# A two-layer mLSTM and RG-LRU trunk on one core: weight-block sums begun later, layer-border splits, sigmoid, gate matrix and head scores moved by half units

## The chip, the cores and the metric

The kernel runs on one core of one Trainium2 chip. The metric is device time in microseconds (us) of one execution. TensorE (PE in the profile) multiplies matrices, VectorE (DVE) and ScalarE (ACT) work elementwise, GpSimd (POOL) does small things and issues accumulating transfers, SyncE (SP) issues most other transfers.

## What is computed

Two layers (`DEPTH`), then a final RMSNorm. The input is 256 tokens of 2048 channels, all in float32.

```
u = rms_norm(x, norm_g)
qk, v, o, z_a, ig, fg, xb, z_b = split(u @ w_in)
qk = silu(causal_dwconv(qk)); q, k = split(qk)       # 8 heads, 128 channels each
h = mlstm_chunkwise(q, k, v, i_pre, log_f) * sigmoid(o)
y_a = head_norm(h) * silu(z_a)
y_b = rg_lru(causal_dwconv(xb) + b, w_a, w_x, lam) * silu(z_b)
x = x + concat(y_a, y_b) @ w_out
```

All but a few per cent of the arithmetic is `u @ w_in` (2048 by 12304) and `@ w_out` (4096 by 2048), twice.

## The kernel before

**Halves.** Float32 products are made of three products of a shorter type (fp32r): each weight tile is split into a rounded part wH and a rest wL, the activations likewise. The unit of work is a *half*: 128x1024 weights of a 1 MB tile `raw` that SP loads. ScalarE casts them to wH (L370), VectorE subtracts to get wL (L371), and TensorE makes 12 products of 512 columns (`mm_a`, L394). There are three `raw` buffers and four wH/wL pairs; a half is prepared three halves ahead (`AHEAD`), and `raw` can be loaded again when wL of its second half is done.

**Order.** `_sequence` lists the weight tiles: per layer four groups `g` of two heads, each with the chunks o, qk, v, xb, z, zb and a gate, and the output chunks of the group before. The loop at L1366 walks through the halves; at each it prepares a later one, emits the products, runs what is due in `timed` (L1392), and calls `pump` (L1395). `pump` advances the generators in `bg`, in which all the work between the products is written. What a generator yields decides: a number is a cost taken from the half's budget, `"wait"` means "not in this half, go on with the next generator", and `None` ends the pump of this half for every generator. Each engine then runs its instructions strictly in the order so made. Instructions that are emitted beside the products are put behind the splits of a certain half on their engine (`Behind`, L102, with `LAG` = 1: the split before the newest).

**Heads.** `qk_post` (L684) sends q and k through a transpose in DRAM (`moved`, `fr`), convolves (12 `qc` steps on VectorE), multiplies by a sigmoid (`qsg`), splits to `qks`, and for each of a group's two heads makes the scores: products into the PSUM tiles `ps_S` (L718, L720), copied and added to `Pt`, which is multiplied by the gate matrix E. Three PSUM banks (`aux`) serve these; a head needs two. `e_gen` (L630) makes E: it loads `nb` from DRAM by GpSimd's queue, yields `None` twice, adds and clips on VectorE (L644), and takes the exponential on ScalarE.

**Border of the layers.** The output chunk `c` of the last group (`out_chunk`, L961) gives the next layer's input: it is transposed through DRAM, and `split` (L1003), due `BORDER` = 7 halves later, scales it, casts it to `x_s` on ScalarE and subtracts on VectorE. The next layer's products read chunk c from the 16th + 4c-th half of the border on.

**Block products.** Two of the chunks, (z, 2) and (o, 3), are multiplied together by a scheme of seven 2x2 block products (`block_halves`, L1088) in place of eight. Their 28 halves per layer have six products each and stand spread between the ordinary ones, in a stretch that begins at `span[l]` (L1344). They need sums of weight blocks, which `weight_sums` (L1064) makes in DRAM: SP copies one block to `w_d` (L1074), GpSimd adds others to it with accumulating transfers (L1076), in quarters of 512 KB, `PACE` = 4 halves apart. It is begun with the first chunk of layer 0.

Of the kernel before, what the change touches and what calls it, by code (L numbers as in the profile page):

```python
# [11 lines left out]
AF = mybir.ActivationFunctionType  # L12
ALU = mybir.AluOpType
# [7 lines left out]
DEPTH = 2  # L21
# [7 lines left out]
LANDING = 4  # L29
BORDER = 7  # L30
BLANKS = 7
PACE = 4
BLOCKS_AHEAD = 5
LAG = 1

# [61 lines left out]
def tile_trunk(ctx, tc, x, xt, par, gw, gb, ws, final_g, out):  # L97
# [4 lines left out]
    class Behind:  # L102
# [4 lines left out]
        def __getattr__(self, name):  # L107
            f = getattr(self.engine, name)

            def g(*a, **k):  # L110
                ins = f(*a, **k)  # L111
                if st.get("behind"):
                    order(ins, done[self.key][-1 - LAG])
                return ins
            return g

# [513 lines left out]
    def e_gen(l, g):  # L630
        while ("nG", l) not in st:
            yield "wait"
        nb = work.tile([P, 2, T], F32, tag="sD", name="nb")
        src = nG_d[l][2 * g : 2 * g + 2, :].rearrange("h t -> (h t)").partition_broadcast(P)
        st["nb", l, g] = nc.gpsimd.dma_start(out=nb.rearrange("p h t -> p (h t)"), in_=src)
        yield None
        yield None
        while ("aT", l) not in st:
            yield "wait"
        E = small.tile([P, 2, 384], F32, tag="E", name="E", bufs=1)  # L640
        aT = st["aT", l]
        for h in range(2):
            hd = 2 * g + h
            ts_(E[:, h, 0:256], nb[:, h, :], aT[:, 0, hd : hd + 1], ALU.add, 0.0, ALU.min)  # L644
            ts_(E[:, h, 256:384], nb[:, h, 128:256], aT[:, 1, hd : hd + 1], ALU.add, 0.0, ALU.min)
        yield 0.7
        order(S.activation(out=E, in_=E, func=AF.Exp), st["wH"])
        for h in range(2):
            for o in (0, 256):
                G.affine_select(out=E[:, h, o : o + 128], in_=E[:, h, o : o + 128], pattern=[[1, 128]],  # L650
                                compare_op=ALU.is_ge, fill=0.0, base=0, channel_multiplier=-1)
        st["E", l, g] = E
        yield 0.1
# [30 lines left out]
    def qk_post(l, g, acc):  # L684
# [3 lines left out]
        def gen():  # L688
# [6 lines left out]
            for ct in range(4):  # L695
                conv(ch, qc, ct, O_QKW + 4 * (8 * (ct % 2) + 2 * g + ct // 2), l, None)
                yield 1.2
            S.activation(out=sg, in_=qc, func=AF.Sigmoid)
            tt_(qc, qc, sg, ALU.mult)
            yield 1.2  # L700
            while ("aT", l) not in st:
# [11 lines left out]
            for h in range(2):  # L713
                pa, pb = aux("ps_S"), aux("ps_S")
                kH, kL = q[:, 2 * h + 1, 0], q[:, 2 * h + 1, 1]
                for ps, ss_, ts_1 in ((pa, slice(0, 128), slice(0, 256)), (pb, slice(128, 256), slice(128, 256))):
                    n_ = ts_1.stop - ts_1.start
                    PE.matmul(ps[:, 0 : 2 * n_].rearrange("p (a t) -> p a t", a=2), kH[:, ss_], q[:, 2 * h, :, ts_1],  # L718
                              start=True, stop=False, skip_group_check=True)
                    PE.matmul(ps[:, 0:n_], kL[:, ss_], q[:, 2 * h, 0, ts_1], start=False, stop=True,  # L720
                              skip_group_check=True)
                for ps, o_, n_ in ((pa, 0, 256), (pb, 256, 128)):
                    S.copy(out=Pt[:, h, o_ : o_ + n_], in_=ps[:, n_ : 2 * n_])
                    tt_(Pt[:, h, o_ : o_ + n_], ps[:, 0:n_], Pt[:, h, o_ : o_ + n_], ALU.add)
                stt(Pt[:, h, :], Pt[:, h, :], DK_SCALE, E[:, h, :], ALU.mult, ALU.mult)
                yield 0.5
            st["scores", l, g] = True
            PH = work.tile([P, 2, 384], F32R, tag="sD", name="PH")
            PL = work.tile([P, 2, 384], F32R, tag="sC", name="PL")
# [231 lines left out]
    def out_chunk(l, g, c):  # L961
# [9 lines left out]
        def postfn():  # L971
            ps = acc()
            if g < NG - 1:
                stage = act.tile([P, 2, 512], F32, tag="stage", name="stage")
                S.copy(out=stage, in_=ps)
                st["gq"] = G.dma_start(out=xd[c], in_=stage, accum_op=ALU.add)
                return
            if c == 0:
                new_ss()
                new_xT()  # L980
                load_gw(l + 1)
            if c % 2:
                two = work.tile([P, 2, 1024], F32, tag="xcs", name="tokblk")
                tok = two[:, 0].rearrange("p (m c t j) -> p m c t j", m=4, c=4, t=2)
                blk = two[:, 1].rearrange("p (m n) -> p m n", m=4)
            else:
                tok, blk = new_tok(), None
            xs = xa(c)
            if c == 3:
                tt_(xs, xs, ps, ALU.add)  # L990
            for t in range(2):
                xt_ = xa(c, t).rearrange("p (c m j) -> p c m j", c=4, m=4)
                if c == 3:
                    S.copy(out=by_block(tok, t), in_=xt_)
                else:
                    tt_(by_block(tok, t), xt_, ps[:, t, :].rearrange("p (c m j) -> p c m j", c=4, m=4), ALU.add)
            if c < 3:
                tt_(xs, xs, ps, ALU.add)
            fr = swapped(tok, blk)
            square_sum(c)  # L1000
            store_x(c)

            def split():  # L1003
                xn = st["x_n"][:, 4 * c : 4 * c + 4]
                split_channels(fr, pars[:, l + 1, O_NG + 4 * c : O_NG + 4 * c + 4], xn[:, :, 0, :], xn[:, :, 1, :])
                st["xT", l + 1, c] = True
            timed.append((st["n"] + BORDER, split))

        for half_src in range(2):
            key = ("ya", l, g) if half_src == 0 else ("yb", l, g)  # L1010
# [52 lines left out]

    def weight_sums():  # L1064

        def moved(l, to, start, r, c, no=None):
            for j in range(2):
                for h in range(2):
                    while no and ("loaded", l, no, 2 * j + h) not in st:
                        yield "wait"  # L1070
                    cs = slice(1024 * h, 1024 * h + 1024)
                    src = block_unit(l, r, c, j)[:, cs]
                    if start:
                        order(nc.sync.dma_start(out=wd[l][to][j][:, cs], in_=src), st["ld"])  # L1074
                    else:
                        order(G.dma_start(out=wd[l][to][j][:, cs], in_=src, accum_op=ALU.add), st["gq"])  # L1076
                    for _ in range(PACE):
                        yield "wait"

        for l in range(DEPTH):  # L1080
            yield from moved(l, 1, True, 1, 1)
            yield from moved(l, 1, False, 0, 1)
            yield from moved(l, 0, True, 0, 0)
            yield from moved(l, 0, False, 0, 1)
            yield from moved(l, 0, False, 1, 1, 5)
            yield from moved(l, 0, False, 1, 0, 6)

    def block_halves(l):  # L1088
        box = {}
# [248 lines left out]
    for item, j in seq:  # L1338
        l, what = item[1], item[2:]
        if _blockwise(item):  # L1340
            if what == PAIR[0]:
                span[l] = (span[l][0], len(order_))
            continue
        if (item[0], what) == ("in", ("qk", 1)) and l not in span:  # L1344
            span[l] = (len(order_), None)
        order_ += [dict(hf, at=(item, j)) for hf in units[item][j]]
    for l in reversed(range(DEPTH)):
# [143 lines left out]
```

## Time and profile before

| | |
|---|---|
| three runs | 1491.24, 1497.0, 1497.49 us, median 1497.0 us |
| profiled execution | 1494.89 us, of which the span of the core's instructions is 1493.2 us |
| granted TensorE clock | 0.998 |
| TensorE / VectorE / ScalarE busy | 99% / 77% / 65% |
| mean rate of the transfers | 257 GB/s |

A row of the grouped views names the line, the engine, the operation and what it writes and reads (out<-in); then the count, the busy time, the mean of one in ns and the idle time before it with what ended it. Where a helper records the instruction, the line is L111 for all of VectorE's and ScalarE's work, so the tile names tell them apart. In a timeline, the number in square brackets is the engine's idle time before the instruction, and what ended it. PE's rows are pipelined: the next product begins before the end of the row before.

### The profile page before, as it was taken

How to read it: one execution, taken by the hardware profiler on the slowest of the kernel's cores; microseconds unless marked ns; L12 is line 12 of the kernel's file. 1: busy time of each engine (PE TensorE's matmuls, PEld its weight loads, DVE VectorE, ACT ScalarE, POOL GpSimd, SP SyncE). 2: the span in 40 equal slices, each digit the busy share in tenths (PEclk: the TensorE clock that was granted, in tenths of full speed). 3: DMA queues.
4: the chain of work that ended last, by engine and by line, in shares of the span. 5: the costliest groups of instructions: out<-in, count | busy, mean ns of one | idle time of the engine just before them, and what ended most of it. 6: DMA issues, size and time to landing. Idle time of an engine off the chain costs nothing.

```text
span 1493.2 us, 18858 instructions
## 1 busy us (share of the span) xinstructions
PE 1475.0 (99%) x6782; PEld 1226.1 (82%) x6782; DVE 1145.7 (77%) x1616; ACT 967.0 (65%) x1258; POOL 104.4 (7%) x186
## 2 busy tenths in 40 slices
PE   9999999999999999999999999999999999999997
PEld 7888788888888888888878788888888888888886
DVE  5787897688787776778867789966787877757775
ACT  7665775567665765658565568756666558655675
POOL 0010010000100101000000100000001000000002
PEclk9999999999999999999999999999999999999999
DMA  9979688898988988986786567778889678778773
GB/s 339 338 224 292 222 301 263 260 293 262 290 290 257 289 300 269 276 265 208 268 286 197 186 217 232 256 237 254 277 264 295 227 229 249 241 228 268 231 270 123
DMA packets 104046, 383.44 MB, mean 257 GB/s; under 512 B 11392, under 2 KB 31888, under 8 KB 84496
## 3 DMA queue, kind: packets, MB, share of 16 engines
q1 hardware_dynamic: 87536, 327.41, 63.7%
q0 software_dynamic: 13952, 50.35, 15.3%
q10 hardware_dynamic: 2464, 4.47, 0.8%
q8 instruction: 53, 0.87, 0.2%
q14 instruction: 41, 0.34, 0.1%
HBM read 344.95 MB, written 62.41 MB: 273 GB/s over the span
## 4 chain that ended last, share of the span: by engine, by line
PE 78%; DMA 5%; ACT 4%; DVE 3%; issue 3%; SPq 0%; ACTq 0%; POOL 0%; DVEq 0%; POOLq 0%
PE acc L394 65%; PE ps_gt L834 2%; DMA raw<-in_ws_dram 2%; PE ps_b L1137 2%; PE ps_b L1138 2%; PE ps_b L1139 2%; DMA x_d<-stage 1%; DVE wL L111 1%; PE acc L407 1%; DMA fr<-moved 1%; ACT wH L111 1%; ACT gate L111 1%; PE acc L1232 1%; PE acc L1231 1%; PE acc L1233 1%
## 5 line engine op out<-in xcount | busy, mean ns | idle before, releaser
L394 PE MATMUL acc<-wH,x_s 128*128 128x512 f32 x2752 | 859.2, 389 | 1.7 <-ACT wH L111 1.7
L111 DVE TENSOR_TENSOR wL<-raw,wH 128x1024 fp32r<-128x1024 f32 (+1 forms) x500 | 597.2, 1202 | 221.1 <-ACT wH L111 219.6
L111 ACT CAST wH<-raw 128x1024 fp32r<-128x1024 f32 (+1 forms) x500 | 515.2, 1038 | 337.4 <-PE acc L394 278.2
L394 PEld LDWEIGHTS acc<-wH,x_s 128*128 128x128 f32 x2752 | 516.5, 188 | 108.8 <-ACT wH L111 2.5
L394 PE MATMUL acc<-wL,x_s 128*128 128x512 f32 x1376 | 535.1, 390 | 4.2 <-DVE wL L111 4.0
L394 PEld LDWEIGHTS acc<-wL,x_s 128*128 128x128 f32 x1376 | 258.3, 188 | 60.2 <-DVE wL L111 7.2
L111 ACT ACT_TABLE_LOAD x60 | 77.0, 1283 | 16.4 <-DVE qc L111 7.8
L394 PE MATMUL acc<-wH,ybH 128*128 128x512 f32 x224 | 87.3, 390 | 0.1
L394 PE MATMUL acc<-wH,yaH 128*128 128x512 f32 x224 | 87.3, 390 | 0.0
L394 PE MATMUL acc<-wH,yaL 128*128 128x512 f32 x224 | 87.3, 390 | 0.0
L394 PE MATMUL acc<-wH,ybL 128*128 128x512 f32 x224 | 87.1, 390 | 0.1
L394 PE MATMUL acc<-wL,yaH 128*128 128x512 f32 x224 | 87.2, 389 | 0.0
L394 PE MATMUL acc<-wL,ybH 128*128 128x512 f32 x224 | 87.2, 389 | 0.0
L111 DVE TENSOR_TENSOR wL<-rawb,wH 128x1024 fp32r<-128x1024 f32 x56 | 68.3, 1220 | 15.7 <-ACT wH L111 14.7
L111 ACT CAST wH<-rawb 128x1024 fp32r<-128x1024 f32 x56 | 58.9, 1052 | 25.8 <-PE acc L394 11.2
L515 POOL DMA_DIRECT2D fr<-moved x34 | 19.5, 575 | 493.4 <-DMA moved<-blk 434.8
L111 DVE STREAM_TRANSPOSE blk<-tok 128x1024 f32<-128x1024 f32 x33 | 41.0, 1241 | 11.3 <-ACT tok L111 10.8
L394 PEld LDWEIGHTS acc<-wH,ybL 128*128 128x128 f32 x224 | 42.0, 188 | 9.3 <-DVE ybL L111 0.6
L394 PEld LDWEIGHTS acc<-wH,ybH 128*128 128x128 f32 x224 | 42.1, 188 | 9.2 <-ACT ybH L111 0.6
L394 PEld LDWEIGHTS acc<-wH,yaL 128*128 128x128 f32 x224 | 42.1, 188 | 8.7
L394 PEld LDWEIGHTS acc<-wL,ybH 128*128 128x128 f32 x224 | 42.0, 188 | 8.6
L394 PEld LDWEIGHTS acc<-wL,yaH 128*128 128x128 f32 x224 | 42.1, 188 | 8.4
(217 smaller groups left out, 1619.6 us busy)
## 6 DMA issues: line engine op xcount, KB each, us to landing
raw<-in_ws_dram SPq DMA_DIRECT2D x152, 1024.0 KB, 6.2
raw<-in_ws_dram SPq DMA_DIRECT2D x190, 512.0 KB, 6.0
fr<-moved POOLq DMA_DIRECT2D x34, 512.0 KB, 5.8
moved<-blk SPq DMA_DIRECT2D x132, 128.0 KB, 2.8
w_d<-in_ws_dram POOLq DMA_DIRECT2D x32, 512.0 KB, 11.7
rawb<-w_d SPq DMA_DIRECT2D x32, 512.0 KB, 5.8
rawb<-in_ws_dram SPq DMA_DIRECT2D x24, 512.0 KB, 6.6
x_d<-stage POOLq DMA_DIRECT2D x24, 512.0 KB, 7.5
```

What stands on the lines that cost most here:

```text
L111: ins = f(*a, **k)
L394: st["mm"] = PE.matmul(o, a_[:, kt, P * t : P * t + P], W[:, k], start=b, stop=z)
L407: PE.matmul(ps[:, ct, T * part : 2 * T], W[:, k, P * ct : P * ct + P], moving, start=first and k == 0 and part == 0, stop=last and k == 3 ...
L515: i0 = back.dma_start(out=fr.rearrange("p a c t i -> p a (c t i)"), in_=moved)
L834: PE.matmul(o, W[:, ib, jl], xs[:, ib, a, :], start=j == 0 and i == 0 and W is Hv and a == 0, stop=i == 1 and W is Lv, skip_group_check=True)
L1137: PE.matmul(box["b"], aH, Hv[:, k], start=kp == 0 and k == 0, stop=False)
L1138: PE.matmul(box["b"], aH, Lv[:, k], start=False, stop=False)
L1139: PE.matmul(box["b"], aL, Hv[:, k], start=False, stop=kp == 3 and k == 1)
L1231: PE.matmul(o, yH[:, kt, tsl], Hv[:, k, cs], start=start and k == 0, stop=False)
L1232: PE.matmul(o, yH[:, kt, tsl], Lv[:, k, cs], start=False, stop=False)
L1233: PE.matmul(o, yL[:, kt, tsl], Hv[:, k, cs], start=False, stop=stop and k == 1)
```

## The change

1. The sums of weight blocks begin when the first group's heads of layer 0 are done (`"hn", 0, 0`) and not with the first chunk; copy and first addition alternate quarter by quarter; the pace is 3 halves and not 4.
2. The border splits of chunks 1 to 3 are due one half later, and are put behind the newest half's wH and wL (`lag` 0) and not behind those of the half before.
3. q/k's sigmoid is put behind the newest wH.
4. E waits for four halves behind the load of `nb`, where it stopped everything else for two.
5. The second head's scores come a half later than the first's.
6. In layer 0 the stretch of the block products begins at (o, 1), 8 halves later than at (qk, 1).

```
-PACE = 4
+PACE = 3
...
-                    order(ins, done[self.key][-1 - LAG])
+                    order(ins, done[self.key][-1 - st.get("lag", LAG)])
...
-        yield None
-        yield None
+        for _ in range(4):
+            yield "wait"
         while ("aT", l) not in st:
             yield "wait"
         E = small.tile([P, 2, 384], F32, tag="E", name="E", bufs=1)
...
-            S.activation(out=sg, in_=qc, func=AF.Sigmoid)
+            order(S.activation(out=sg, in_=qc, func=AF.Sigmoid), st["wH"])
...
                 stt(Pt[:, h, :], Pt[:, h, :], DK_SCALE, E[:, h, :], ALU.mult, ALU.mult)
                 yield 0.5
+                if h == 0:
+                    yield "wait"
...
             def split():
+                st["lag"] = 0
                 xn = st["x_n"][:, 4 * c : 4 * c + 4]
                 split_channels(fr, pars[:, l + 1, O_NG + 4 * c : O_NG + 4 * c + 4], xn[:, :, 0, :], xn[:, :, 1, :])
                 st["xT", l + 1, c] = True
-            timed.append((st["n"] + BORDER, split))
+                st["lag"] = LAG
+            timed.append((st["n"] + BORDER + (c > 0), split))
...
+        parts = [(j, h) for j in range(2) for h in range(2)]
+        while ("hn", 0, 0) not in st:
+            yield "wait"
+        for l in range(DEPTH):
+            for to, a, b in ((1, (1, 1), (0, 1)), (0, (0, 0), (0, 1))):
+                for at in parts:
+                    yield from moved(l, to, True, *a, *at)
+                    yield from moved(l, to, False, *b, *at)
...
-        if (item[0], what) == ("in", ("qk", 1)) and l not in span:
+        if (item[0], what) == ("in", ("qk" if l else "o", 1)) and l not in span:
```

Three places show what this does to the engines' queues. SyncE in layer 0, around the end of the first group's xb chunk (`raw` is a weight tile, `moved` the transpose through DRAM, `w_d` a copy of a block for the sums). Before:

```order
L330 DMA raw_1133<-in_ws_dram 128x2048
L514 DMA moved_1177<-blk_1174 32x4x256 x4
L330 DMA raw_1212<-in_ws_dram 128x2048
L328 DMA raw_1290<-in_ws_dram 128x1024 x2
L328 DMA raw_1330<-in_ws_dram 128x1024 x2
L328 DMA raw_1366<-in_ws_dram 128x1024 x2
L328 DMA raw_1421<-in_ws_dram 128x1024 x2
L514 DMA moved_1415<-blk_1412 32x4x256 x4
L330 DMA raw_1504<-in_ws_dram 128x2048
```

and now:

```order
L330 DMA raw_1132<-in_ws_dram 128x2048
L514 DMA moved_1193<-blk_1190 32x4x256 x4
L330 DMA raw_1226<-in_ws_dram 128x2048
L1074 DMA w_d010_123<-in_ws_dram 128x1024
L328 DMA raw_1285<-in_ws_dram 128x1024 x2
L328 DMA raw_1325<-in_ws_dram 128x1024 x2
L328 DMA raw_1361<-in_ws_dram 128x1024 x2
L328 DMA raw_1416<-in_ws_dram 128x1024 x2
L1074 DMA w_d010_123<-in_ws_dram 128x1024
L514 DMA moved_1410<-blk_1407 32x4x256 x4
L330 DMA raw_1499<-in_ws_dram 128x2048
```

The first two of layer 0's eight copies now stand here; before, five of the eight stood ahead of these rows. On GpSimd's queue the addition that follows each copy has moved with it.

ScalarE at the border of the layers (`tok` scales chunk 1 of the next input, `x_s` is its cast, `tokblk` belongs to chunk 3). Before:

```order
L111 CAST wH_6435<-raw_6321 128x1024
L111 CAST wH_6454<-raw_6321 128x1024
L111 ACTIVATE tok_6470<-fr_6308,pars_105 128x256 x4
L111 CAST wH_6477<-raw_6356 128x1024
L111 CAST x_s_6249<-tok_6470 128x4x256
L111 COPY tokblk_6493<-x_acc_5853 128x4x4x32 x2
```

and now:

```order
L111 CAST wH_6435<-raw_6321 128x1024
L111 CAST wH_6454<-raw_6321 128x1024
L111 CAST wH_6470<-raw_6356 128x1024
L111 ACTIVATE tok_6503<-fr_6308,pars_105 128x256 x4
L111 CAST wH_6512<-raw_6356 128x1024
L111 CAST x_s_6249<-tok_6503 128x4x256
L111 COPY tokblk_6486<-x_acc_5853 128x4x4x32 x2
```

One more wH has moved ahead of the step that waits for the transpose, and the next one ahead of `tokblk`.

VectorE in the first group of layer 1, where E is made. Before:

```order
L111 SCALAR_TENSOR_TENSOR qc_7163<-ch_7161,pars_105,qc_7163 128x255
L111 SCALAR_TENSOR_TENSOR qc_7163<-ch_7161,pars_105,qc_7163 128x254
L111 TENSOR_SCALAR E_7079<-nb_7022,at0_7049 128x256
L111 TENSOR_SCALAR E_7079<-nb_7022,at0_7049 128x128
L111 TENSOR_SCALAR E_7079<-nb_7022,at0_7049 128x256
L111 TENSOR_SCALAR E_7079<-nb_7022,at0_7049 128x128
L111 TENSOR_TENSOR wL_7170<-raw_7059,wH_7169 128x1024
L111 SCALAR_TENSOR_TENSOR qc_7163<-ch_7161,pars_105,qc_7163 128x253
L111 SCALAR_TENSOR_TENSOR qc_7163<-ch_7161,pars_105,qc_7163 128x255
L111 SCALAR_TENSOR_TENSOR qc_7163<-ch_7161,pars_105,qc_7163 128x254
L111 TENSOR_TENSOR wL_7193<-raw_7059,wH_7192 128x1024
```

and now:

```order
L111 SCALAR_TENSOR_TENSOR qc_7144<-ch_7126,pars_105,qc_7144 128x253
L111 SCALAR_TENSOR_TENSOR qc_7144<-ch_7126,pars_105,qc_7144 128x254
L111 TENSOR_TENSOR wL_7174<-raw_7061,wH_7173 128x1024
L111 TENSOR_SCALAR E_7116<-nb_7022,at0_7049 128x256
L111 TENSOR_SCALAR E_7116<-nb_7022,at0_7049 128x128
L111 TENSOR_SCALAR E_7116<-nb_7022,at0_7049 128x256
L111 TENSOR_SCALAR E_7116<-nb_7022,at0_7049 128x128
L111 SCALAR_TENSOR_TENSOR qc_7144<-ch_7126,pars_105,qc_7144 128x253
L111 SCALAR_TENSOR_TENSOR qc_7144<-ch_7126,pars_105,qc_7144 128x255
L111 TENSOR_TENSOR wL_7197<-raw_7061,wH_7196 128x1024
L111 SCALAR_TENSOR_TENSOR qc_7144<-ch_7126,pars_105,qc_7144 128x254
```

wL of the half has moved ahead of E, and of the twelve `qc` steps four remain behind E where seven did.

More of the change, by code (lines that the diff above doesn't have):

```diff
@@ L1064, in weight_sums, with moved @@
     def weight_sums():
[L1066 to L1069, printed above, removed]
-                        yield "wait"
[L1071 to L1086, printed above, removed]
+        def moved(l, to, start, r, c, j, h):
+            cs = slice(1024 * h, 1024 * h + 1024)
+            src = block_unit(l, r, c, j)[:, cs]
+            if start:
+                order(nc.sync.dma_start(out=wd[l][to][j][:, cs], in_=src), st["ld"])
+            else:
+                order(G.dma_start(out=wd[l][to][j][:, cs], in_=src, accum_op=ALU.add), st["gq"])
+            for _ in range(PACE):
+                yield "wait"
+        parts = [(j, h) for j in range(2) for h in range(2)]
+        while ("hn", 0, 0) not in st:
+            yield "wait"
+        for l in range(DEPTH):
[3 more added lines that the diff above has]
+                    yield from moved(l, to, False, *b, *at)
+            for no, a in ((5, (1, 1)), (6, (1, 0))):
+                for j, h in parts:
+                    while ("loaded", l, no, 2 * j + h) not in st:
+                        yield "wait"
+                    yield from moved(l, 0, False, *a, j, h)
     def block_halves(l):
```

## The prediction

> **What bounds the kernel now.** The page comes first: busy times, then the costliest groups of TensorE and VectorE.
>
> ```profile
> PE 1475.0 (99%) x6782; PEld 1226.1 (82%) x6782; DVE 1145.7 (77%) x1616; ACT 967.0 (65%) x1258; POOL 104.4 (7%) x186
> ...
> L394 PE MATMUL acc<-wH,x_s 128*128 128x512 f32 x2752 | 859.2, 389 | 1.7 <-ACT wH L111 1.7
> L111 DVE TENSOR_TENSOR wL<-raw,wH 128x1024 fp32r<-128x1024 f32 (+1 forms) x500 | 597.2, 1202 | 221.1 <-ACT wH L111 219.6
> ```
>
> TensorE is the bound, and its 6782 products stay: the change moves work and takes no product away. So all that can be won is the time in which PE stands still. The chain of waits gives the true pace of a product.
>
> ```profile
> 184.67 8.16 PE acc L394 x36
> ```
>
> 36 products in 8.16 us are 0.227 us each, while its group above records 0.389: rows overlap by 0.16. A recorded idle time I therefore means that PE lost I + 0.16, and another 0.11 where the row behind it is 0.50 long and not 0.39. I use I + 0.27. Next, the waits of PE, by tile (us in total, times, longest):
>
> ```profile
> PE acc L394 <- DVE wL L111: 4.0, 6, 1.2
> PE acc L394 <- ACT wH L111: 1.7, 2, 1.4
> PE ps_gt L834 <- ACT gate L111: 1.6, 1, 1.6
> ...
> PE ps_S L718 <- DVE Pt L111: 0.7, 1, 0.7
> ```
>
> These ten are few and single, so each has a place. The timeline of PE names them:
>
> ```profile
> 152.58 0.50 PE L834 MATMUL ps_gt<-xcs,wH 128*128 128x256 f32 x2 [1.65 <-ACT gate L111]
> ...
> 177.81 0.50 PE L394 MATMUL acc<-wL,x_s 128*128 128x512 f32 x1 [1.18 <-DVE wL L111]
> ...
> 629.91 0.38 PE L718 MATMUL ps_S<-qks 128*128 128x256 f32 x1 [0.68 <-DVE Pt L111]
> ...
> 752.64 0.50 PE L394 MATMUL acc<-wL,x_s 128*128 128x512 f32 x1 [0.53 <-DVE wL L111]
> ...
> 755.69 0.50 PE L394 MATMUL acc<-wH,x_s 128*128 128x512 f32 x1 [0.26 <-ACT wH L111]
> 756.95 0.50 PE L394 MATMUL acc<-wL,x_s 128*128 128x512 f32 x1 [0.76 <-DVE wL L111]
> ...
> 849.50 0.50 PE L394 MATMUL acc<-wH,x_s 128*128 128x512 f32 x1 [1.41 <-ACT wH L111]
> 850.95 0.50 PE L394 MATMUL acc<-wL,x_s 128*128 128x512 f32 x1 [0.95 <-DVE wL L111]
> ```
>
> By I + 0.27 the gate at 152.58 costs 1.9 us, the wL at 177.81 1.45, the border of the layers (752 to 757) 0.80 + 0.53 + 1.03 = 2.4, layer 1's first heads (849 to 851) 1.68 + 1.22 = 2.9, and the scores at 629.91 0.95. The change is aimed at just these.
>
> **Part 1, the sums.** The gate's chain, then GpSimd's timeline:
>
> ```profile
> 136.10 11.02 DMA raw<-in_ws_dram
> ...
> 162.71 8.21 DMA raw<-in_ws_dram
> ```
>
> ```profile
> 132.85 1.75 POOL L1076 DMA_DIRECT2D w_d<-in_ws_dram  x2
> ...
> 161.45 0.88 POOL L1076 DMA_DIRECT2D w_d<-in_ws_dram  x1
> ```
>
> The page's table of transfers gives what a load takes as a rule:
>
> ```profile
> raw<-in_ws_dram SPq DMA_DIRECT2D x190, 512.0 KB, 6.0
> ```
>
> A load that meets two additions takes 11.02 us, one that meets a single addition 8.21, the usual one 6.0. In the changed order one copy and one addition stand where two additions stood, so I price the load at 136.10 at 8.21: it lands 2.8 us earlier, more than the 1.9 that the gate cost PE. ScalarE shows that nothing else held it there:
>
> ```profile
> 147.22 1.05 ACT L111 CAST wH<-raw 128x1024 fp32r<-128x1024 f32 x1 [5.02 <-DMA raw<-in_ws_dram]
> ```
>
> From this wH a table load, two sz and one wH lead on ScalarE to the gate that PE has at 152.58, and all come 2.8 us sooner. **Taken: 1.9.** Ends: 0, if copy and addition cost as two additions do, and 1.9.
>
> The addition at 161.45 stays where it was, so the load at 162.71 stays at some 8.2 us. What changes is VectorE's order: before, yaL stood ahead of the wL for which PE waits at 177.81, and waited for yaH; now this wL stands ahead of yaL.
>
> ```profile
> 174.81 1.22 DVE L111 TENSOR_TENSOR yaL<-tok,yaH 128x1024 fp32r<-128x1024 f32 x1 [1.70 <-ACT yaH L111]
> ```
>
> That is 1.70 + 1.22 us less ahead of it, against 1.45 lost. But yaL then stands ahead of the following wL, and PE arrives 1.9 earlier while the load doesn't. **Taken: 0.8** of 1.45, about the middle.
>
> **Part 2, the border.** ScalarE's timeline:
>
> ```profile
> 748.68 1.71 ACT L111 ACTIVATE tok<-fr,pars 128x256 f32<-128x256 f32 x4 [3.36 <-DMA fr<-moved]
> 750.29 1.04 ACT L111 CAST wH<-raw 128x1024 fp32r<-128x1024 f32 x1
> ...
> 754.61 2.93 ACT L111 CAST wH<-raw 128x1024 fp32r<-128x1024 f32 x3
> ```
>
> ScalarE stands 3.36 us for the transpose with a wH queued behind it; tok, x_s and pieces of chunk 3 then push a further wH to 754.61. Moving one wH of 1.04 us into the idle time of 3.36, and a second ahead of tokblk, removes all three waits of PE. What it could cost is x_s:
>
> ```profile
> 752.51 1.22 DVE L111 TENSOR_TENSOR x_s<-tok,x_s 128x1024 fp32r<-128x1024 f32 x1
> ```
>
> ```profile
> 746.28 0.39 PE L394 MATMUL acc<-wH,x_s 128*128 128x512 f32 x1
> ```
>
> Chunk 1 is done at 753.7. PE begins layer 1 at 746.28 and wants chunk 1 four halves later, a half being 12 x 0.227 = 2.7 us: 757.2 if nothing stops it. That is 3.5 us of cover, and tok still begins when the transpose lands, so at most the half of 2.7 is used up. **Taken: 2.2 of 2.4**, 0.2 kept for what is left of the last wL.
>
> **Parts 3 and 4, q/k's sigmoid and E.** VectorE and ScalarE in layer 1:
>
> ```profile
> 837.33 1.01 DVE L111 TENSOR_SCALAR E<-nb,at 128x256 f32<-128x256 f32 x4 [4.18 <-DMA nb<-nG_d]
> ...
> 839.38 1.48 DVE L111 SCALAR_TENSOR_TENSOR qc<-ch,pars,qc 128x253 f32<-128x253 f32 x3
> ```
>
> ```profile
> 845.01 1.28 ACT L111 ACT_TABLE_LOAD   x1 [3.49 <-DVE qc L111]
> 846.30 1.06 ACT L111 ACTIVATE qsg<-qc 128x1024 f32<-128x1024 f32 x1
> 847.27 1.25 ACT L111 ACTIVATE tok<-acc,rstd 128x512 f32<-128x512 f32 x2
> 848.40 1.99 ACT L111 CAST wH<-raw 128x1024 fp32r<-128x1024 f32 x2
> ```
>
> E waits 4.18 us for nb with wL and seven qc behind it; ScalarE then waits 3.49 for the last qc, and table load, qsg and tok stand ahead of the wH that PE lacks at 849.50. In the new order a wL and three qc use VectorE's idle time. Four qc (1.48 for three, so 2.0) and one wL (1.2) remain behind E. Even if nb lands 0.9 later, because its place is behind more, E ends at 839.2, the last qc at 842.4, and 1.28 + 1.06 + 1.25 later, at 846.0, the wH can begin: 2.4 sooner than 848.40, where PE lacked 1.68. The wL for 850.95 hangs on the same steps and also comes 2.4 to 2.6 sooner, where 1.68 + 1.22 = 2.9 are wanted. **Taken: 2.5 of 2.9.** The same moves in layer 0's first heads, where no wait of this kind stands in PE's list, may cost 0.3 through more qc between two splits: 2.2 in all. The ends are 0 (if nb comes 2.5 later still) and 2.9.
>
> **Part 5, the scores.** The costs beside 629.91 hide in rows without a wait:
>
> ```profile
> 112.60 0.39 PE L394 MATMUL acc<-wL,x_s 128*128 128x512 f32 x1
> 112.98 0.39 PE L718 MATMUL ps_S<-qks 128*128 128x256 f32 x1
> 113.20 0.22 PE L720 MATMUL ps_S<-qks 128*128 128x128 f32 x1
> ```
>
> From 112.60 to 112.98 are 0.38 and not 0.227, and the score of 256 columns keeps its successor for 0.22 and not half of 0.227: 0.26 us, for the second head's bank that is not yet free. Eight groups have this, one at 0.95: 0.95 + 7 x 0.26 = 2.8. A half of 2.7 us is ten times the 0.26 that the bank came late. **Taken: 2.4**, between 0 (if the second head then meets other users of the banks) and 2.8.
>
> **What is late next.** Part 6 and the new order put some three qc steps more ahead of a wL of the stretch behind 174 us, which is VectorE's: by windows (us, then busy PE, PEld, DVE, ACT, POOL),
>
> ```profile
> 174.00:238.00 64.00, 62.83 (x277) 51.57 (x276) 59.70 (x87) 46.01 (x58) 4.43 (x9) 1.00 0.82 279
> ```
>
> 59.70 of 64 us are busy there, and one wL is just in time:
>
> ```profile
> 217.43 1.22 DVE L111 TENSOR_TENSOR wL<-raw,wH 128x1024 fp32r<-128x1024 f32 x1
> ```
>
> ```profile
> 218.74 0.47 PE L394 MATMUL acc<-wL,x_s 128*128 128x512 f32 x1
> ```
>
> It ends at 218.65, 0.09 before PE. Three qc more ahead of it are 1.5 us; nothing excludes that other work moves off in exchange, so the ends are 0 and 1.5, and with so small a margin I take 1.0. For other waits that surface as PE comes earlier I take 0.5, the size of the smaller ones above.
>
> **The sum.** Removed: 1.9 + 0.8 + 2.2 + 2.2 + 2.4 = 9.5. New: 1.5. Net 8.0 us of the span of 1493.2, which gives 1485.2; the profiled execution lay 1.7 around its span, so 1486.9 against 1494.9. The median of the three runs stands 2.1 above that execution and the fastest 3.7 below it; I add half of the 2.1: **1488.0**. A measurement of this kernel can tell about 0.5% (7.5 us) from no change, so faster means below 1489.5, slower above 1504.5.
>
> **Rivals.** *VectorE's stretch takes back what was won ahead of it.* All that PE wins before 174 us (1.9, 0.8, and 0.4 of scores) and the 1.5 of qc go into later wL in 174 to 238, less the 1.0 booked: 3.6 more, **1491.6**. For it: 59.70 of 64. Against: 4.3 us are free, and a VectorE that starts earlier keeps its lead.
>
> *Everything goes and nothing new appears.* 1.9 + 1.45 + 2.4 + 2.9 + 2.8 = 11.4, **1484.6**. Taken off 1493.2 and with 2.8 added as above. Against: the margin of 0.09.
>
> *A single addition costs a load as much as two do.* If the queue of the load and that of the additions share the engines turn by turn, it is the number of queues with work and not of transfers that counts; the load at 136.10 then stays at 11 us and the gate's 1.9 remain: **1489.9**. Against: 8.21 with one, 11.02 with two. The Trainium skill ("DMA: Bandwidth & Descriptors", section "Queues, rings and completion order") says that each DMA engine alternates between the queues that have work, a packet from each, which is this rival's rule; the two loads here do not bear it out, as far as two can.
>
> *Slower: the crowd of sums.* All eight copies and eight additions of layer 0 now fall behind some 129 us, where five copies stood ahead of it. If each pair makes a load late enough to stop PE as at 152.58, for 1.9, and the gate's and the wL's 2.7 stay as well, the time is 1488.0 + 2.7 + 1.9 n for n such pairs: 1500 for n = 5, 1506 for all eight. It is slower than before from n = 4. For it: the stretch from 174 to 238 moves 279 GB/s already, with the DMA engines busy for 0.82 of the time. Against: 0.18 of them are free, three of the eight copies stood in this stretch before, and the addition at 161.45, alone, cost its load 2.2 us, which is less than the two together cost (5.0).
>
> **How the numbers follow.** Forecast 0.50 (its own range 1485 to 1491); taken back 0.24; everything 0.12; one addition as two 0.05; the crowd 0.09. Below 1489.5 lie three quarters of the forecast's cases (0.37), all of "everything" (0.12), and 0.06 of "taken back" and "one addition as two": faster 0.55. Above 1504.5 lies the crowd with all eight pairs, or with fewer of which some stop PE twice, something under half of its 0.09: slower 0.04. The rest, 0.41, is the same. The range from 1482.5 (everything, with 2 us for the spread of the runs) to 1496 (taken back, with 2 for the spread, and the crowd with up to two pairs, 1494.5) leaves out under 2 in 10.
>
> **What would show it.** Right: the first load behind the group's xb chunk takes about 8 us and the gate comes without a wait of PE; PE has no wait for wH or wL in the first halves of layer 1 nor in its first heads, and none for Pt. Wrong: waits of PE for wL between 200 and 240 of over 2 us in all (the first rival); a load behind 129 us of over 9 us with a wait of PE behind it (the crowd); the first group's load still at 11 us (one addition as two); PE waiting for x_s at the border.

## The result, and the profile after

| | before | changed |
|---|---|---|
| first comparison, median of 20 runs each | 1496.99 us | 1490.05 us (1486.64 to 1495.76) |
| ratio | | 0.9959, 95% interval 0.9948 to 0.9969 |
| a later comparison, 11 and 6 runs | 1498.93 us | 1488.07 us (1487.62 to 1489.72) |
| ratio | | 0.9935, 95% interval 0.992 to 0.995 |
| profiled execution | 1494.89 us, span 1493.2 | 1488.34 us, span 1486.6 |

The kernel became 0.4% faster in the first comparison and 0.65% in the second: 6 to 10 us by these ratios, where 9.0 was forecast. By the prediction's own line, below 1489.5, the first median counts as the same (0.41 was given to it) and the second as faster (0.55). The total came out near 1488; the terms behind it did not all.

The page of the changed kernel first, then the waits of PE by tile (us in total, times, longest):

```profile
PE 1471.1 (99%) x6782; PEld 1225.6 (82%) x6782; DVE 1147.7 (77%) x1616; ACT 967.0 (65%) x1260; POOL 115.6 (8%) x186
```

```profile
PE acc L394 <- DVE wL L111: 2.9, 4, 1.5
PE acc L394 <- ACT wH L111: 1.4, 3, 0.6
PE ps_blank L144 <- DVE blank L111: 1.3, 1, 1.3
PE ps_n L656 <- DVE dn L111: 1.2, 1, 1.2
```

The 6782 products are the same. The waits for the gate and for Pt are gone from the list, and a wait for `dn`, which nobody had named, is new. The timeline of PE shows where the larger of the remaining waits lie:

```profile
124.14 0.36 PE L656 MATMUL ps_n<-vH,PH 128*128 128x258 f32 x1 [1.15 <-DVE dn L111]
...
230.83 0.50 PE L394 MATMUL acc<-wL,ybH 128*128 128x512 f32 x1 [0.35 <-DVE wL L111]
...
533.67 0.50 PE L394 MATMUL acc<-wH,x_s 128*128 128x512 f32 x1 [0.49 <-ACT wH L111]
...
534.93 0.50 PE L394 MATMUL acc<-wL,x_s 128*128 128x512 f32 x1 [0.76 <-DVE wL L111]
...
539.53 0.50 PE L394 MATMUL acc<-wL,x_s 128*128 128x512 f32 x1 [1.54 <-DVE wL L111]
```

None of these stood in before's list. Every wait that the prediction priced is gone, and others have come. Two windows say where that leaves the kernel (us, then the busy time of PE and the other engines). Before:

```profile
0.00:560.00 560.00, 555.40 (x2531) 460.84 (x2532) 437.22 (x647) 367.74 (x485) 46.79 (x86) 1.00 0.87 281
560.00:960.00 400.00, 394.83 (x1828) 327.21 (x1827) 312.50 (x444) 261.55 (x346) 22.45 (x48) 1.00 0.74 242
```

and changed:

```profile
0.00:560.00 560.00, 553.53 (x2529) 459.45 (x2530) 435.80 (x646) 367.19 (x486) 52.45 (x88) 1.00 0.88 285
560.00:960.00 400.00, 399.41 (x1856) 332.72 (x1855) 319.69 (x453) 263.56 (x349) 25.74 (x46) 1.00 0.71 239
```

Up to 560 us PE does 2531 products before and 2529 now: nothing is won there. From 560 to 960 it does 1828 and 1856; 28 more products at 0.227 us are 6.4 us, nearly the whole difference of the spans (6.6). The gain is that of the border and of layer 1's first heads (5.3 us by the prediction's pricing), with the wait for Pt at 629.91. The gate, the wL behind it and the sums' part brought about as much in the first 200 us as was lost again by 560.

### The profile page after: what moved, and what is told of

It is laid out like the page before. It is cut to its first block, busy times and chain, and to the rows that moved or that the text cites. A ratio compares the mean times of both kernels' runs of the same rounds, so it can differ in the third digit from the quotient of the medians.

```text
span 1486.6 us, 18865 instructions
## 1 busy us (share of the span) xinstructions
PE 1471.1 (99%) x6782; PEld 1225.6 (82%) x6782; DVE 1147.7 (77%) x1616; ACT 967.0 (65%) x1260; POOL 115.6 (8%) x186
## 4 chain that ended last, share of the span: by engine, by line
PE 80%; DVE 5%; DMA 3%; ACT 3%; issue 1%; SPq 0%; ACTq 0%; DVEq 0%; POOLq 0%
PE acc L394 67%; PE ps_gt L836 2%; DVE wL L111 2%; PE ps_b L1143 2%; PE ps_b L1144 2%; PE ps_b L1145 2%; DMA raw<-in_ws_dram 1%; PE acc L407 1%; DMA fr<-moved 1%; DMA moved<-blk 1%; ACT wH L111 1%; ACT L111 1%; PE acc L1239 1%; PE acc L1237 1%; PE acc L1238 1%
## 5 line engine op out<-in xcount | busy, mean ns | idle before, releaser
L111 DVE STREAM_TRANSPOSE blk<-tok 128x1024 f32<-128x1024 f32 x33 | 41.0, 1241 | 12.5 <-ACT tok L111 12.0
L394 PEld LDWEIGHTS acc<-wH,yaH 128*128 128x128 f32 x224 | 42.0, 188 | 8.6
```

Source lines behind the costliest of these rows:

```text
L394: st["mm"] = PE.matmul(o, a_[:, kt, P * t : P * t + P], W[:, k], start=b, stop=z)
```

## Experiments

Two theories on the new stop at 533 to 540, which costs 0.65 + 1.15 + 1.82 = 3.6 us by the starts of the products. Theory 1: an addition of the sums now lies beside a transpose through DRAM and makes it slow. Theory 2: PE has won 3 us by then, and meets a transpose that takes the time it always took. The changed kernel's rows there, SyncE, GpSimd, ScalarE and VectorE:

```profile
512.03 2.47 SPq L514 DMA_DIRECT2D moved<-blk  x4
```

```profile
509.79 0.85 POOL L1076 DMA_DIRECT2D w_d<-in_ws_dram  x1 [9.94 <-DMA w_d<-in_ws_dram]
510.32 1.21 POOL L978 DMA_DIRECT2D x_d<-stage  x1
522.88 0.56 POOL L515 DMA_DIRECT2D fr<-moved  x1 [11.34 <-DMA moved<-blk]
```

```profile
530.98 1.71 ACT L111 ACTIVATE tok<-fr,pars 128x256 f32<-128x256 f32 x4 [5.01 <-DMA fr<-moved]
```

```profile
533.65 1.23 DVE L111 TENSOR_TENSOR wL<-raw,wH 128x1024 fp32r<-128x1024 f32 x1 [4.28 <-ACT wH L111]
```

ScalarE waits 5.01 us for the transpose, a wH stands queued behind tok, and VectorE waits 4.28 for that wH: the pattern that the border had before. From the issue of the transpose (512.03) to tok (530.98) are 18.95 us. The addition was issued 2.2 us ahead of it.

**The old sums in the changed kernel.**

```
-PACE = 3
+PACE = 4
...
-        while ("hn", 0, 0) not in st:
-            yield "wait"
...
+            yield from moved(l, 1, True, 1, 1)
+            yield from moved(l, 1, False, 0, 1)
+            yield from moved(l, 0, True, 0, 0)
+            yield from moved(l, 0, False, 0, 1)
```

> The changed kernel with the sums of weight blocks as they were before (begun with the first chunk, pace 4). Open is the new stop of PE between 533 and 540 us, 3.6 us in all, where yaH and a wH come late behind a transpose through DRAM. Theory 1: a copy, an addition and the x_d store queued behind that addition now meet this transpose. Then the stop is gone here (under 0.5 us left), and in exchange the wait for the gate near 152 us comes back with 1.6 to 1.9; the time is about 1488 to 1490. Theory 2: the transpose takes as long as it takes, and any kernel in which PE has won 3 us by then runs into it. Then 3 us or more of waits stay between 525 and 545, the gate's wait comes back as well, and the time is about 1492.

Measured 1494.64 us, ratio 0.9982 (0.9972 to 0.9991), 2.6 us more than theory 2 said and over 4 more than theory 1. PE's timeline:

```profile
92.90 0.50 PE L394 MATMUL acc<-wL,x_s 128*128 128x512 f32 x1 [2.32 <-DVE wL L111]
...
157.15 0.50 PE L836 MATMUL ps_gt<-xcs,wH 128*128 128x256 f32 x2 [3.01 <-ACT gate L111]
...
183.61 0.50 PE L394 MATMUL acc<-wL,x_s 128*128 128x512 f32 x1 [1.43 <-DVE wL L111]
```

The gate's wait is back, and longer; the wL of 177.81 is back; and at 92.90 there is a stop that neither kernel has. There VectorE waits for nb:

```profile
90.31 1.01 DVE L111 TENSOR_SCALAR E<-nb,at 128x256 f32<-128x256 f32 x4 [5.11 <-DMA nb<-nG_d]
```

The stop at 533 is gone, but PE is 5 us later by then than in before, so this run doesn't tell the theories apart. It shows that the rest of the change brings less with the old sums (0.9982) than with the new ones (0.9959); the stop at 92.90 itself does not come when only the border, E and the sigmoid are changed (below).

**The new sums alone, on before.**

```
-PACE = 4
+PACE = 3
...
+        while ("hn", 0, 0) not in st:
+            yield "wait"
+        for l in range(DEPTH):
+            for to, a, b in ((1, (1, 1), (0, 1)), (0, (0, 0), (0, 1))):
+                for at in parts:
+                    yield from moved(l, to, True, *a, *at)
+                    yield from moved(l, to, False, *b, *at)
```

> The kernel before with the new sums alone (begun behind the first group's heads, piece by piece, pace 3). Prediction's step: the gate's wait of 1.65 us near 152 is gone, since one addition lies beside its load and not two. The wait for wL at 177.81 (1.18) stays, if it hangs on the place of yaL, which part 6 and not the sums moved. Theory 1: a stop of 1 to 4 us appears near 530 to 545 us, and the time is 1495 to 1498, no gain. Theory 2: PE has won only 1.9 us here, the stop is at most 1 us, and the time is about 1495.

Measured 1497.71 us, ratio 1.0002 (0.9992 to 1.0012): no gain at all. PE's timeline:

```profile
176.46 0.50 PE L394 MATMUL acc<-wL,x_s 128*128 128x512 f32 x1 [2.91 <-DVE wL L111]
...
541.40 0.50 PE L394 MATMUL acc<-wL,x_s 128*128 128x512 f32 x1 [1.59 <-DVE wL L111]
```

The gate's wait is gone, as forecast; the wL behind it takes back 1.7 us more, and the stop near 540 appears (0.43 at 536.80 and this 1.59) although PE has lost as much by then as in before (9.8 us against 10.3, by the starts of the products). That speaks for theory 1. The addition is issued at 511.70, the transpose at 514.51, tok comes at 532.84: 18.3 us.

**The changed kernel at the old pace.**

```
-PACE = 3
+PACE = 4
```

> The changed kernel with a pace of 4 halves in place of 3, so that the additions of layer 1's sums stand elsewhere against the same transposes. Theory 1: the stop of 3.6 us between 533 and 540 is gone or under 1.5, and the time is about 1487, if no other addition meets a transpose. Theory 2: the stop stays at 3 us or more and the time is 1490.

Measured 1492.5 us, ratio 0.9975 (0.9963 to 0.9987). At this pace some block products of layer 0 take sums of weights that are not complete, so this kernel computes other block products. The stop at 533 is gone, with 14.8 us from transpose to tok and no addition for 23 us ahead of it. But the sums, now late, stop PE elsewhere:

```profile
386.31 0.49 PE L1143 MATMUL ps_b<-wH,sums 128*128 128x512 f32 x1 [3.87 <-ACT wH L111]
```

PE is again some 5 us late at 533, so this too is no clean test.

**Both heads' scores in one half.**

```
-                if h == 0:
-                    yield "wait"
```

> The changed kernel without the half between the two heads' scores. Theory: the wait for the bank of ps_n at 124 us (1.3 us) was put there by this half, since it pushes the first head's evacuation beside the second head's products; it is gone here, and the eight small stops at the scores come back, 2.5 us in all against about 0.6: the time is within 1 us of the changed kernel's 1490. Rival: the wait at 124 us comes from PE being earlier or from E's new place; then it stays with 1 us or more, and the time is about 1492.

Measured 1488.89 us, ratio 0.9942 (0.9926 to 0.9958), against 0.9959 (0.9948 to 0.9969) with the half: no difference that can be told. The wait for dn at 124 is gone, and these are back:

```profile
107.42 0.39 PE L718 MATMUL ps_S<-qks 128*128 128x256 f32 x1 [0.59 <-DVE Pt L111]
...
161.73 0.50 PE L394 MATMUL acc<-wL,x_s 128*128 128x512 f32 x1 [0.95 <-DVE wL L111]
```

So the half between the scores takes away small stops in eight groups, and puts a larger one at the products behind them in the first group. The rival, that PE's earliness alone causes the wait at 124, falls: ahead of it PE is as early here as in the kernel at pace 4, which has the half and waits 1.97. But the half alone doesn't bring the wait either: the kernel with the old sums has the half, PE is 3 to 4 us later there, and no such wait shows.

**Block products from (qk, 1) on, as before.**

```
-        if (item[0], what) == ("in", ("qk" if l else "o", 1)) and l not in span:
+        if (item[0], what) == ("in", ("qk", 1)) and l not in span:
```

> The changed kernel with the block products of layer 0 spread from (qk, 1) on as before (part 6 undone). The sums alone had a stop of 2.9 us for wL near 176, where the changed kernel has none. If it is the later begin of the block products that keeps it away, a wait of 1 to 3 us for wL between 170 and 180 comes back here, the wait of 0.4 us at 231 goes, and the time is 1 to 2.5 us above the changed kernel's 1490. If the other parts keep it away (the border of the half at the scores, E), nothing comes back there and the time is within 1 us of 1490.

Measured 1492.01 us, ratio 0.9962 (0.9945 to 0.9978). The wL near 178 has a wait of only 0.16, so part 6 is not what took it away. A new stop lies further on:

```profile
214.47 0.50 PE L1144 MATMUL ps_b<-wL,x_s 128*128 128x512 f32 x1 [1.65 <-DVE wL L111]
```

In the crowded stretch a block product's wL now comes late. Whether part 6 is worth anything in time is not shown: the ratio can't be told from the changed kernel's 0.9959.

**Three pairs of sums held.** The last three pairs of layer 1's second sum wait for the fourth group's heads of layer 0.

```
                 for at in parts:
+                    while (l, to) == (1, 0) and at > (0, 0) and ("hn", 0, 3) not in st:
+                        yield "wait"
                     yield from moved(l, to, True, *a, *at)
```

> The changed kernel with the last three pairs of layer 1's sums held until the fourth group's heads of layer 0 are done, so that no addition is issued between 500 and 600 us. Theory 1 (an addition issued 2 to 3 us ahead of the transpose makes it slow): from the issue of the transpose near 512 to tok some 15 to 16 us and not 19, the stop of 3.6 us between 533 and 540 under 0.7, and the time about 1486.5 to 1487.5. Theory 2 (PE has won 3 us by then, and the transpose takes its time anyway): 2 us or more of the stop stay and the time is 1488.5 or more. A third way: the held pairs stop PE where they now fall, between 640 and 700, and the time is 1490.

Measured 1486.8 us, ratio 0.9928 (0.9912 to 0.9944), the best so far. SyncE, GpSimd and ScalarE at the transpose:

```profile
514.04 2.77 SPq L514 DMA_DIRECT2D moved<-blk  x4
```

```profile
512.39 0.85 POOL L978 DMA_DIRECT2D x_d<-stage  x1 [10.05 <-ACT stage L111]
520.55 0.56 POOL L515 DMA_DIRECT2D fr<-moved  x1 [7.30 <-DMA moved<-blk]
```

```profile
528.46 1.71 ACT L111 ACTIVATE tok<-fr,pars 128x256 f32<-128x256 f32 x4 [0.32 <-DMA fr<-moved]
```

14.4 us from transpose to tok, and the stop is gone. The store `x_d` is still issued beside the transpose, so it was not the store that made it slow. PE has lost 9.3 us by then, as little as with the sums alone (9.8), where a stop of 2.0 us by the records was there with an addition and is not here without: theory 1 holds, for copy and addition together, since both are held. A stop that the first profile of the changed kernel doesn't have shows at 412 us (its cause is told below the table of transposes):

```profile
412.34 0.50 PE L394 MATMUL acc<-wL,x_s 128*128 128x512 f32 x1 [1.40 <-DVE wL L111]
```

**The same, and the first group's scores as before.**

```
-                if h == 0:
+                if h == 0 and (l or g):
```

> As the kernel with the three pairs held, and in the very first group the second head's scores again in the same half as the first's (in all other groups a half later). If the wait of 1.3 us at 124 is put there by that half, and the small stops at the scores of the other groups stay away: 0.5 to 1.3 us less than with the held pairs alone, about 1486. If the wait of 1.3 us at 162 comes back as it did without any such half, no gain against the held pairs alone.

Measured 1485.83 us, ratio 0.9925 (0.9905 to 0.9946): with the kernel above, no difference that can be told. The wait at 124 is gone; 0.58 at 107.44 for Pt and 0.8 us at 161 are back.

**Border, E and q/k's sigmoid alone, on before.**

```
-        yield None
-        yield None
+        for _ in range(4):
+            yield "wait"
...
+            order(S.activation(out=sg, in_=qc, func=AF.Sigmoid), st["wH"])
...
+                st["lag"] = 0
...
+            timed.append((st["n"] + BORDER + (c > 0), split))
```

> The kernel before with parts 2 to 4 alone (border splits, q/k's sigmoid, E). By the prediction's steps the three waits between 752 and 757 (2.4 us) and the two at 849 and 851 (2.9 us) go and everything else stays: about 1492. Rival: with the old sums the copies lie beside nb of the first group in layer 0, and E, held back, brings the stop of 2.3 us at 93 with the slow products behind it (4.2 us in all), seen with the old sums in the changed kernel; then the gain is about 1 us, 1496.

Measured 1493.15 us, ratio 0.9975 (0.9963 to 0.9987): 4.2 us. In layer 1 the waits of the border and of the first heads go but for 0.35 at 761.62. The stop at 93 does not come (0.37 at 91.26), so that rival falls. What comes back lies at the same wL as in before, and larger:

```profile
179.87 0.50 PE L394 MATMUL acc<-wL,x_s 128*128 128x512 f32 x1 [2.24 <-DVE wL L111]
```

**The changed kernel and the held one, once more on one chip.**

> The changed kernel once more, beside the next one on one chip. If its stops have the places that the first profile showed, the waits at 124 (1.2 us) and between 533 and 540 (3.6 us lost) are there again and tok follows the transpose's issue by about 19 us; time 1489 to 1491, 0.995 to 0.997 of before. If those stops were chance of one execution, they are elsewhere.

> The kernel with the three pairs held and the first group's scores as before, once more, beside the changed kernel on one chip. If it is better by what its first profile lost less (10.7 against 12.8 us of stops, so 2 us, and up to 4 by the medians), it takes 1485 to 1488, and 0.9975 to 0.9985 of the changed kernel. If the first comparison was chance, the two lie within 1 us.

The changed kernel took 1488.07 us, 0.9935 (0.992 to 0.995) of before; the one with held pairs and the first group's scores as before 1484.92 us (1483.19 to 1487.91), 0.9913 (0.9894 to 0.9931). In medians the second takes 0.9979 of the first; six runs each, which overlap in one. PE's timeline of the changed kernel in this execution:

```profile
125.31 0.36 PE L656 MATMUL ps_n<-vH,PH 128*128 128x258 f32 x1 [2.16 <-DVE dn L111]
...
179.18 0.50 PE L394 MATMUL acc<-wL,x_s 128*128 128x512 f32 x1 [0.68 <-DVE wL L111]
...
413.57 0.50 PE L394 MATMUL acc<-wL,x_s 128*128 128x512 f32 x1 [1.13 <-DVE wL L111]
```

The wait at 124 is there again, and longer. The one at 533 is not. PE lost 1.0 us more at 124, 1.3 at 413 and 0.8 at 179 ahead of it, and the addition (510.95) was issued 4.3 us ahead of the transpose (515.26) and not 2.2, which then took 15.8 us. The spans of the two executions are 1486.6 and 1486.8: the stops moved, their sum did not. Up to 560 us PE lost 10.5 us in the one and 10.6 in the other (10.3 in before), by the starts of its products. tok comes at 530.98 in one and at 531.02 in the other, at 530.59 in before. So a part of theory 2 holds too: in these two executions tok comes at about 531 wherever PE has lost the time before, and the earlier transpose is the longer one by as much as it is earlier. With the pairs held, tok comes at 527.5 to 528.5, and the waits of PE in the second execution of the held kernel are

```profile
PE acc L394 <- DVE wL L111: 1.4, 3, 0.7
PE ps_blank L144 <- DVE blank L111: 1.3, 1, 1.3
PE acc L394 <- ACT wH L111: 0.9, 1, 0.9
PE ps_S L718 <- DVE Pt L111: 0.6, 1, 0.6
PE ps_rb L465 <- DVE dg L111: 0.4, 1, 0.4
```

This transpose in all executions, from the issue on SyncE to tok on ScalarE:

| kernel | last addition ahead of it | transpose to tok | stop of PE there, recorded |
|---|---|---|---|
| changed | 2.2 us | 18.95 us | 2.8 us |
| sums alone | 2.8 us | 18.3 us | 2.0 us |
| scores in one half | 2.5 us | 19.0 us | 2.4 us |
| block products as before | 3.3 us | 16.5 us | 0.5 us |
| changed, second execution | 4.3 us | 15.8 us | none |
| before; old sums; border and E alone | 12 us | 15.7; 16.0; 15.7 us | none |
| pace 4 | 23 us | 14.8 us | none |
| held (three executions) | over 20 us | 14.0 to 14.4 us | none |

On the whole, the nearer the addition ahead of it, the longer the transpose. The landing times fit this. An addition is on its way for 8.2 to 9.1 us here, so it lay beside the transpose's stores (`moved`) for 6.3 to 6.6 us in the first three rows, 5.0 in the fourth and 3.9 in the fifth; in the others it had landed before. The first store took 9.1 to 9.7 us in the first three rows, then 8.1 and 6.9, and at most 6.1 in the others.

The held kernels leave out a copy as well as an addition. In every kernel of the table but these and the one at pace 4, SyncE issues a copy 3.8 to 5.2 us behind the transpose. Before, the old sums, and the border and E alone have this copy and no near addition, and take 15.7 to 16.0 us; those with neither take 14.0 to 14.8. So about 1.3 us of what holding saves here may be the copy's, and the rest is the addition's.

The stop between 411 and 421 us comes behind a late transpose too, and here one kernel shows both cases. A transpose of layer 0 near 386 us, which ends in `ch` on ScalarE, has an addition ahead of it that waits for a load of the sums, and the two executions of the changed kernel issued this addition at different distances. In the first it came at 377.05, 7.3 us ahead of the transpose (384.39), whose data had landed 11.9 us later. In the second it came at 384.29, 2.4 us ahead of the transpose (386.67), and the data landed 19.4 us later, so that ScalarE waited. PE was 2 us later by then than in the first execution, so its earliness is not the reason.

```profile
406.13 1.05 ACT L111 COPY ch<-fr 128x1024 f32<-128x1024 f32 x1 [2.30 <-DMA fr<-moved]
```

Behind `ch`, VectorE waits for ScalarE, and the wL behind that comes late for PE at 413.57. The two executions of the kernel with held pairs and the first group's scores as before show the same pair: 2.6 us and 18.7 in the one, with a stop of 0.4, and 7.3 us and 12.5 in the other, with none. The kernel with only the pairs held (2.9 us) and the one with the block products as before (2.8 us) took 19.5 us each and have the stop; both heads' scores in one half (6.2 us) took 11.6 and has none. One execution doesn't fit as well: the sums alone, with 2.3 us, took 14.5 and have no stop there.

## Why the prediction was right or wrong

**The total** was right, and the sum behind it had two errors that cancel, so its nearness is in part luck. Of what the change was to remove more went than I took: 12.1 us (the span is 6.6 shorter, with 5.5 new in it), where I had 9.5; 1.0 of it are two small waits for wL, at 102 and 162, that I had left in place. Of what was to appear I had 1.5, and 5.5 came in the first execution.

**The gate: 1.9 taken, 1.9 gone**, and with the new sums alone as well. The load was priced at 8.21 us; it took 6.98 (6.6 is the median of the two loads issued together). The copy must land before its addition can start, so the addition was issued 3.7 us behind the load (134.23) and not ahead of it:

```profile
raw<-in_ws_dram SPq DMA_DIRECT2D x2, 512.0 KB, 6.6
```

```profile
137.94 0.89 POOL L1076 DMA_DIRECT2D w_d<-in_ws_dram  x1 [4.39 <-DMA w_d<-in_ws_dram]
```

The step was right in its outcome and not in its price. The 8.21 is from a load of 1 MB (L330, 128x2048), for which the page of before has a row of its own:

```profile
raw<-in_ws_dram SPq DMA_DIRECT2D x152, 1024.0 KB, 6.2
```

The 11.02 is from the second of two loads of 512 KB that were issued together (L328). So the two do not set one addition against two. With the new sums alone the gate's load did lie beside one addition (134.89), and it took 9.96 us:

```profile
134.03 9.96 DMA raw<-in_ws_dram
```

It landed 3.1 us earlier than in before, 2.1 of them because it was issued earlier, which the prediction did not have and whose cause was not traced. In the changed kernel it landed 5.5 us earlier, 1.5 of them by its issue (134.64).

The rival that one addition costs as much as two is wrong in its outcome, as the gate's 1.9 went. Its rule is not tested by the changed kernel's load, since the addition came behind it. Beside one addition the next two loads of 512 KB took 9.20 and 9.98 us there, and the gate's load 9.96 with the sums alone; beside two it took 11.02 in before and 14.26 in the kernel with the old sums. So two cost more than one in these executions, by 1 to 4 us, and one costs more than was taken. The 1 MB load of the wL behind the gate, with one addition beside it, took 8.69 us now (8.21 before). The Trainium skill ("DMA: Bandwidth & Descriptors", section "Queues, rings and completion order") says that each DMA engine takes the queues that have work in turn, a packet from each. These loads do not settle whether the number of queues alone sets the price.

**The wL at 177.81: 0.8 taken, 1.45 gone** (0.8 of it back in the second execution). The mechanism was right, but the order alone doesn't decide: in four kernels in which yaL stands ahead of this wL in VectorE's order (before, old sums, sums alone, border and E alone) PE waits 1.18, 1.43, 2.91 and 2.24 us; in those in which it stands behind, 0 to 0.7. At pace 4 yaL stands ahead as well and PE waits for nothing there: yaL has no wait for yaH (1.70 in before), and PE is 2 us later. It takes the new sums together with E's new place or that of q/k's sigmoid (these two were not run apart) to turn the order. Neither the sums alone nor parts 2 to 4 alone do. Undoing part 5 or part 6 does not turn it back; the old pace does.

**The border: 2.2 taken, 2.4 gone. First heads of layer 1: 2.5 taken, 2.9 gone.** VectorE and ScalarE of the changed kernel, against the rows of before with 4.18 and 3.49:

```profile
834.10 1.01 DVE L111 TENSOR_SCALAR E<-nb,at 128x256 f32<-128x256 f32 x4 [2.08 <-DMA nb<-nG_d]
```

```profile
838.05 1.28 ACT L111 ACT_TABLE_LOAD   x1 [1.12 <-DVE qc L111]
...
841.45 1.04 ACT L111 CAST wH<-raw 128x1024 fp32r<-128x1024 f32 x1
```

E waits half as long for nb and ScalarE a third as long for the last qc. The loss of 0.3 that I set against it in layer 0 did not come: the small wait at 102 went as well.

**The scores: 2.4 taken, about 2.5 gone, and 1.3 to 2.3 put in their place** at 124. In before seven groups had the stop and not eight: 0.95 and six times 0.26. My ends were 0 and 2.8, with the reason "if the second head then meets other users of the banks". That is what happened, a stage later: it is ps_n, the next user of the same banks, that waits in the first group. Net, the runs with and without this part can't be told apart.

**The stretch 174 to 238: 1.0 taken, 0.6 lost**, at 230.83 and not at 218.74. The rival that this stretch takes everything back was wrong in the place and right in the outcome: what was won ahead of 200 us was gone by 560.

**The step that failed** is "For other waits that surface as PE comes earlier I take 0.5": 4.9 us came at 124 and 533 in the first execution, 4.4 at 124, 179 and 413 in the second. The additions were followed only through layer 0's stretch (the rival of the crowd). Layer 1's sums, which the pace moved as well, were not followed, nor were the additions' neighbours other than weight loads. The transpose at 512 takes 18.3 to 19.0 us with an addition issued 2 to 3 us ahead of it, against 15.7 to 16.0 with none near, and ScalarE's queue passes that on to wH.

What stays open: by which resource an addition holds up a transpose, why the sums alone got off lightly at 386 us, and why the half between the scores brings the wait at 124 only with the new sums. That an addition made the gate's stop in before rests on before, the new sums alone and the old sums; it was not tried with the additions taken out, and an earlier issue of the load has a part in it.

## What to carry to other kernels

Follow a moved background transfer past all neighbours on its way, in later stages too, and not only past the loads of weights; here one addition of 512 KB beside a transpose cost PE 3.6 us, about what the change had won up to there. Where such a transfer waits for another one, its distance to its neighbours can differ between two executions of one kernel, so read more than one profile. In an in-order queue the instruction that waits for such a transfer should stand behind the work that is ready: the border, E and the sigmoid alone brought 4.2 of the 6 to 10 us. And a stop taken away early is worth only as much as the next supply that has not moved allows, so compare the count of products up to a common time, not the list of waits.

## What the runs showed of the hardware

Some stops cost more than their length. In the kernel with the old sums, the windows behind the stops at 92.90 and 157.15 (the column of 0.50 and 0.57 is the granted clock):

```profile
94.00:96.00 2.00, 2.00 (x7) 1.52 (x6) 2.00 (x5) 0.08 (x1) 1.08 (x2) 0.50 0.79 242
158.00:162.00 4.00, 4.00 (x16) 3.32 (x15) 3.97 (x5) 3.97 (x8) 0.00 (x0) 0.57 0.76 259
```

For some 3 us a product takes 0.43 us and not 0.227, which adds 1.4 to 1.7 us to a stop of 2.3 to 3.0. The same came behind 2.24 us at 179.87 with the border and E alone and behind 3.87 at pace 4, but not behind 2.91 (sums alone), 2.16 (changed, second execution) or 2.06 (block products as before). So the length alone doesn't decide. The Trainium skill ("TensorE: Matmul & The Clock Gate", section "Part 1: The HAM clock gate (the "warmup" mystery)") says that the clock is halved behind an idle window of about 3.4 us, and that these windows run freely. That the halving depends on where a stop falls agrees with the free-running windows; that 2.24 us were enough does not agree with a window that is idle throughout.
